# Layer 1's output projection for tokens 0 to 1015 as seven quarter products, and empty side steps ahead of the modulation's column sums

## The chip, the cores and the metric

One core of a Trainium2 chip runs the whole program. The metric is device microseconds of one execution. Before the change the median of three runs is 2443.7 us (2438.36 to 2445.88).

## The reference

A stream x of 2048 tokens with 1024 features passes two layers and a final RMSNorm, all in float32. Each layer computes `h = rmsnorm(x) * (1 + scale) + shift`, a mixer of width 2048 on h, and adds `gate * y`. Shift, scale and gate (3072 numbers a layer) are `silu(c) @ ada_w[i] + ada_b[i]`.

- Layer 0: `u, v, gate = split(h @ w_in)`, then `y = (gelu(u) * spatial(layernorm(gelu(v))) * silu(gate)) @ gmlp_w_out`, where spatial mixes tokens inside chunks of 128.
- Layer 1: `p, gate = split(h @ w_in)`, p has its windowed mean (2, 4, 8 or 16 tokens) taken off, is mixed within four groups and scaled, and `y = (mixed * silu(gate)) @ pool_w_out`.

`pool_w_out` is 2048 x 1024. Its product for the first 1016 tokens is what the change touches.

## The kernel before

**Data.** Features lie on the 128 partitions and tokens on the free axis. Every float32 product is three matmuls (`mm3`, L103) of a high and a low fp32r part: hi*hi, hi*lo, lo*hi. `put` (L109) makes the two parts of a 512-wide piece with one ACT cast (L111) and one DVE subtraction (L112), into one of 9 pairs of tiles.

**Passes.** The tokens are worked in two passes of 1024. A layer's input projection in a pass is 8 groups c of two *units*, and a unit (`unit`, L677) is seven products of quarters (Strassen-like: two halves of the tokens times two halves of the output features, with sums of weights and of rows) of 12 matmuls 128x512 each. Layer 0's stages are the fused weights (`fuse`), `v_phase`, `b_phase0` (L928, both units plus the spatial mixing, PE tile `psp`) and `c_phase0` (L1036), each of the last three once a pass. Layer 1's are `b_phase1` (L1143) and the output projection.

**The two forms of the output projection.** `c_pairs` (L999) serves layer 0: a pass has seven products (order CORDER = 1, 2, 6, 5, 7, 3, 4), each of 8 steps k, each step 4 output blocks times 3 matmuls: 672 matmuls. A step's operands (a piece of y or of a sum of y's quarters, and a piece of weights or of a sum of weights) are two loads into one `raw` tile and two `put`s. After each product four DVE instructions (L1014) add the bank, times the gate, onto the fetched rows of x. The sums of y's quarters are made in `row_sums` (L921), those of the weights in `sum_quarters` (L733: four loads, four DVE subtractions, four stores, all loads and stores on POOL's queue). `c_phase` (L970) serves layer 1's first 1016 tokens: two calls of 508 tokens with all 16 pieces c, 8 output blocks and 3 matmuls: 384 matmuls a call, 768 together. There y's piece is read into a `g` tile. The remaining 1032 tokens go through a third form at the end that the change leaves alone.

**Side steps.** Work that has no place of its own waits in a queue `side`. In `b_phase0` and `b_phase1` the queue is served after every product: one step after each of the 7 products of the first unit, two after each of the second, so 21 a group and 168 a pass. From the second group on, the first step of a group in `b_phase0` is the `row_sums` of the group before, which leaves 161 for the queue. What is left after the last group is run at once by `do_side()` (L958), ahead of `c_phase0`. A `rest` is a step that does nothing.

**The modulation's column sums.** `ada_late` (L470) computes 512 of the 3072 numbers in ten steps: one that issues the first load; eight that each multiply one loaded 128x512 piece of `ada_w` (tile `x`, two of them) by a number of c and add it to `ra` (one tile; L454, L456, DVE); and `last`, in which PE adds up the partitions with 8 matmuls into a bank `pm` (L462) and DVE adds the bias (L464). The loads go on SP's queue behind the weight stream. Pass 0 of `b_phase0` holds five such groups behind 54 steps of RMS norms and 56 of `sum_quarters`, pass 1 three behind 72.

**Order.** Each engine has one list of instructions, fixed when the program is compiled: by and large the order of the text, where an instruction whose operands or buffers are not there yet in the compiler's reckoning lets later ones pass. The stream of weight loads (`Stream`, L33) makes pieces four jobs ahead and loads LEAD (4, in `c_pairs` 8) jobs beyond, as far as `raw` tiles are free: 6 in layer 0, 4 in layer 1.

The functions that the diff touches:

Of the kernel before, what the change touches and what calls it, by code (L numbers as in the profile page):

```python
# [17 lines left out]
P = 128  # L18
# [45 lines left out]
def hybrid_kernel(ctx: ExitStack, tc: tile.TileContext, a: dict):  # L64
# [13 lines left out]
    v_d = dram.tile([2, 8, P, 8, 2 * P], F32, name="v_d")  # L78
    y_d = dram.tile([2, 8, 7, P, TB], F32, name="y_d")
    to_d = dram.tile([8, 2, P, W2], F32, name="to_d")  # L80
    y1_d = dram.tile([NC, P, L], F32, name="y1_d")
    bt_d = dram.tile([8, P, 2 * P], F32, name="bt_d")

    BIG = {"A": 6, "V": 4, "Q": 2, "X": 2}
# [7 lines left out]
    def work(tag, width=512):  # L92
        return wk.tile([P, WK[tag][0]], F32, name=tag, tag=tag, bufs=WK[tag][1])[:, 0:width]
# [4 lines left out]
    def part(pair, *idx):  # L98
        return tuple(t[idx] for t in pair)
# [23 lines left out]
    def st_load(dst, src):  # L123
        st.last = nc.sync.dma_start(dst, src).ins

    def load(dst, src):

        with tc.issue_after(st.last):
            nc.sync.dma_start(dst, src)

    def new_pair():
        return (pair_pool.tile([P, 512], F32R, name="whi", tag="whi"),
                pair_pool.tile([P, 512], F32R, name="wlo", tag="wlo"))
# [4 lines left out]
        return RAW["pool"].tile([P, W2], F32, name="raw", tag="raw")  # L138

    def split(src):  # L140
        p = new_pair()
        put(p, src)
        return p

    def half_jobs(src, step=W2):

        box = []

        def load():
            box.append(raw_tile())  # L150
            for o in range(0, W2, step):
                st_load(box[0][:, o:o + step], src()[:, o:o + step])

        return (load, lambda: split(box[0][:, 0:512])), (None, lambda: split(box[0][:, 512:W2]))
# [138 lines left out]

    CORDER = (1, 2, 6, 5, 7, 3, 4)

    def co_jobs(y, w, t):

        src = {1: lambda k: w(k, 0)[:, 0:512], 2: lambda k: w(k, 1)[:, 0:512], 3: lambda k: w(k, 1)[:, 512:W2],
               5: lambda k: t[k, 0][:, 0:512], 7: lambda k: t[k, 0][:, 512:W2],
               4: lambda k: t[k, 1][:, 0:512], 6: lambda k: t[k, 1][:, 512:W2]}  # L300

        def two(k, pn):
            box = []

            def load():
                box.append(raw_tile())
                st_load(box[0][:, 0:512], y(k, pn))
                st_load(box[0][:, 512:W2], src[pn](k))

            return (load, lambda: split(box[0][:, 0:512])), (None, lambda: split(box[0][:, 512:W2]))  # L310

        return {pn: [st.add(*two(k, pn)) for k in range(8)] for pn in CORDER}

    def c_jobs(y, w):

        jobs = []
        for c in range(0, NC, 2):
            h = [half_jobs(lambda c=c: w[c]) for c in (c, c + 1)]
            i = st.add(y(c), h[0][0], y(c + 1), h[1][0], h[0][1], h[1][1])
            jobs.append(((i[0], i[2]), (i[1], i[3]), (i[4], i[5])))  # L320
        return jobs

    def c0_jobs(pb):
        return co_jobs(lambda k, pn: y_d[pb, k, pn - 1], lambda k, h: a["g_wo"][2 * k + h], to_d)

    def y1_job(c, t0, n, pair):
        box = []

        def load():
            box.append(work("g", n))  # L330
            st_load(box[0], y1_d[c, :, t0:t0 + n])

        def make():
            p = pair()
            put(p, box[0])
            return p

        return load, make

    def c1_jobs(t0, n):  # L340
        return c_jobs(lambda c: y1_job(c, t0, n, lambda: part(new_pair(), every, slice(0, n))), a["p_wo"])

    def c2_jobs(t0, n):

# [29 lines left out]
        return [two_units(unit_jobs_made(c, partial(wf, c)),  # L374
                          unit_jobs(lambda kh, c=c: a["p_wg"][c, kh]), False) for c in range(8)]

    FIRST = ((0, 508), (508, 508))
    jpg = [pg_jobs()]
    jc1 = [c1_jobs(*s) for s in FIRST]
    jpg.append(pg_jobs())  # L380
    jc2 = [c2_jobs(*s) for s in LAST]

# [42 lines left out]
    def ahead(n, fetch, places=2):  # L425

        got = []

        def get(i):
            while len(got) < min(n, i + 1 + places):  # L430
                got.append(fetch(len(got)))
            return got[i]

        return get
# [33 lines left out]
        return [partial(row, 0)] + [partial(step, k) for k in range(KD)] + [last]  # L468

    def ada_late(i, *gs):  # L470
        return [f for g in gs for f in ada_steps(i, g, 4, lambda: work("x"), lambda: work("ra"))]

    def rsqrt(out, v, tmp):
        pw, cols = v.shape
# [492 lines left out]
            nc.scalar.activation(t, po, AF.Copy, scale=g)  # L967
            nc.vector.tensor_add(x, x, t)

    def c_phase(jobs, t0, n, x_src, gate, tag, store):  # L970

        st.ahead = 4
        po = []
        pace = (len(side) + NC - 5) // (NC - 4)

        def fetch(d):
            x = work("x" if d % 4 < 2 else tag, n)
            load(x, x_src[d, :, t0:t0 + n])
            return x

        row = ahead(KD, fetch, 4)
        for c2, (iy, *iw) in enumerate(jobs):
            for d in range(KD):
                if c2 == 0:
                    po.append(bank("po"))
                for j in range(2):
                    w, y = st.get(iw[d // 4][j]), st.get(iy[j])
                    mm3(po[d][:, 0:n], part(w, every, slice((d % 4) * P, (d % 4 + 1) * P)), y,
                        c2 + j == 0, c2 + j == NC // 2)
                if d % 4 == 3:  # L990
                    do_side(pace)
            if c2 == NC // 2 - 2:
                row(0)
        for d in range(KD):
            x = row(d)
            residual(d, x, po[d][:, 0:n], gate)
            nc.gpsimd.dma_start(store[d, :, t0:t0 + n], x)

    def c_pairs(jobs, tokens, n, x_src, gate, tiles, store):  # L999

        st.ahead, st.LEAD = 4, 8
        total, steps = len(side), 0
        xs, pa, pv = {}, [], []

        def fetch(h, nh, tags):
            for i in range(4):
                x = work(tags[i], n)
                nc.gpsimd.dma_start(x, x_src[nh * 4 + i, :, tokens[h]:tokens[h] + n])
                xs[h, nh, i] = x

        def onto(h, nh, banks, last):
            for i in range(4):
                d, x = nh * 4 + i, xs[h, nh, i]
                nc.vector.scalar_tensor_tensor(x, banks[i][:, 0:n], gate[:, 16 + d:17 + d], x, ALU.mult, ALU.add)  # L1014
                if last:
                    nc.gpsimd.dma_start(store[d, :, tokens[h]:tokens[h] + n], x)

        use = {1: ((0, 0), 0), 2: ((0, 0), 1), 6: ((0, 1), 0), 5: ((1, 1), 0), 7: ((1, 1), 1), 3: ((0, 1), 1), 4: ((1, 0), 1)}
        begin = {1: 0, 6: 0, 5: 1, 4: 1}
        for pn in CORDER:  # L1020
            chain = pa if pn in (1, 6, 7, 4) else pv
            if pn in (1, 2, 5):
                chain[:] = [bank("po") for _ in range(4)]
            for k in range(8):
                y, w = (st.get(i) for i in jobs[pn][k])
                for i in range(4):
                    mm3(chain[i][:, 0:n], part(w, every, slice(i * P, (i + 1) * P)), part(y, every, slice(0, n)),
                        k == 0, k == 7, pn in (6, 7, 4, 3))
                if k == 3 and pn in begin:
                    fetch(*use[pn][0], tiles[begin[pn]])  # L1030
                steps += 1
                do_side(total * steps // 56 - (total - len(side)))
            onto(*use[pn][0], chain, use[pn][1])
        st.LEAD = 4
# [3 lines left out]


    tsum = [sum_quarters(t_d[c], partial(wf, c)) for c in range(8)]  # L1040
    tsum_o = [sum_quarters(to_d[k], lambda h, k=k: a["g_wo"][2 * k + h]) for k in range(8)]


# [21 lines left out]
    for b in (0, 1):  # L1065
        rms, steps = fetched_rms(src1(b), TB, "ra", "x", 8)
        rms1.append(rms)
        side.extend(steps)
    side.extend(ada_late(1, 12, 16, 20))
    b_phase0(1, rows, stats)  # L1070
    rows = Rows(1, [src1(0), src1(1)], rms1)
    sums = rows.sum_steps(lambda: work("g"))
# [53 lines left out]
            w *= 2  # L1126
        return steps + [last]

    def gated(bb, c, pc, g1, g2):

        s, y = psc[:, c:c + 1], pc[:, 16:W2 + 16]
        n2 = TB - 8 if bb == 0 else TB
        nc.vector.scalar_tensor_tensor(y[:, 0:TB], y[:, 0:TB], s, g1, ALU.mult, ALU.mult)
        nc.vector.scalar_tensor_tensor(y[:, TB:TB + n2], y[:, TB:TB + n2], s, g2[:, 0:n2], ALU.mult, ALU.mult)
        if bb == 0:
            nc.gpsimd.tensor_copy(keep_g[:, c, :], g2[:, n2:TB])
            nc.gpsimd.dma_start(y1_d[c, :, 0:W2 - 8], pc[:, 16:W2 + 8])
        else:
            e = pc[:, 8:16]
            nc.vector.scalar_tensor_tensor(e, e, s, keep_g[:, c, :], ALU.mult, ALU.mult)  # L1140
            nc.gpsimd.dma_start(y1_d[c, :, W2 - 8:L], pc[:, 8:W2 + 16])

    def b_phase1(bb, rows):  # L1143
        st.ahead = 4
        for c in range(8):
# [25 lines left out]
            g = unit(rows, jpg[bb][c][1], gt, gate)  # L1171
            for pn in ORDER:
                g(pn, 2)
            side.extendleft(partial(gated, bb, c + 8 * i, pcs[i], gt[i], gt[2 + i]) for i in (1, 0))
        do_side()

    def final_out(rms, x, d, t0, n, eng):
# [19 lines left out]
        return wide.pop()  # L1197

    sums = rows.sum_steps(half_wide)
    side.extend(sums[:8])  # L1200
    c_phase(jc1[0], *FIRST[0], x1_d, mod[1], "g", x2_d)
    side.extend(sums[8:])
    c_phase(jc1[1], *FIRST[1], x1_d, mod[1], "g", x2_d)

    def final_steps(t0, n):

# [100 lines left out]
```

## Time and profile before

| | us |
|---|---|
| median of the runs | 2443.7 |
| lowest, highest | 2438.36, 2445.88 |
| the profiled execution | 2437.09 |
| its span | 2435.3 |
| PE busy in it | 2391.0 |
| DVE busy in it | 1932.7 |

The span runs from the first to the last instruction; 1.8 us of the profiled execution lie around it. Times of the trace are microseconds from the span's start. `b_phase0` lies at 280 to 638 and 950 to 1292, `c_phase0` at 642 to 798 and 1292 to 1444, `b_phase1(0)` at 1444 to 1753, the two calls of `c_phase` at 1753 to 1929, `b_phase1(1)` at 1929 to 2237.

### The profile page before, as it was taken

Reading aid. Unit: us, or ns where it says so; the run is one execution under the profiler, and the core shown is the slowest. Engines: PE = TensorE matmul, PEld = TensorE weight load, DVE = VectorE, ACT = ScalarE, POOL = GpSimd, SP = SyncE. Lnnn points to the kernel's source line nnn. Section 1 sums busy time; section 2 is a strip of 40 time slices with the busy share of each in tenths; the row PEclk is TensorE's granted clock in tenths of the full one; section 3 lists DMA queues with packets and bytes.
Section 4 is the critical chain, followed back from the end, with each engine's and each line's share of the span. In section 5 each row is a group of like instructions: output and inputs, shape, how many; then the busy total and the mean of one; then the engine's idle time right before and its main releaser. Section 6 shows DMA issues by size and latency. Waiting matters only on the chain.

```text
span 2435.3 us, 33160 instructions
## 1 busy us (share of the span) xinstructions
PE 2391.0 (98%) x11200; PEld 2014.6 (83%) x11200; DVE 1932.7 (79%) x3231; ACT 1089.4 (45%) x1878; POOL 338.2 (14%) x622
## 2 busy tenths in 40 slices
PE   8999999989999999999999999999999999999998
PEld 7768888868788888888888888888888888888998
DVE  6786789988897677888978869888875498988655
ACT  5744554433465444444446643333354333323533
POOL 2211112321101242010101011010001001100011
PEclk9999999999999999999999999999999999999999
DMA  9733445776778566345536874332566545446664
GB/s 353 260 127 122 144 141 182 240 236 211 259 252 283 183 228 220 135 161 180 172 129 230 259 236 139 121 117 87 165 185 222 179 142 181 143 130 176 224 194 144
DMA packets 191706, 456.21 MB, mean 187 GB/s; under 512 B 24736, under 2 KB 49312, under 8 KB 190512
## 3 DMA queue, kind: packets, MB, share of 16 engines
q1 hardware_dynamic: 148176, 314.02, 40.6%
q0 software_dynamic: 39328, 135.33, 15.5%
q10 hardware_dynamic: 4032, 4.75, 0.6%
q8 instruction: 88, 1.44, 0.3%
q14 instruction: 82, 0.67, 0.1%
HBM read 343.93 MB, written 110.07 MB: 186 GB/s over the span
## 4 chain that ended last, share of the span: by engine, by line
PE 84%; DVE 6%; DMA 6%; issue 2%; ACT 1%; SPq 0%; POOL 0%; DVEq 0%; POOLq 0%; ACTq 0%
PE pu L105 15%; PE pu L107 15%; PE pu L106 15%; PE po L105 9%; PE po L107 9%; PE po L106 9%; PE pa L105 2%; PE pa L106 2%; PE pa L107 2%; PE psp L908 2%; PE pv L107 1%; PE pv L105 1%; PE pv L106 1%; DVE wlo L112 1%; DMA x<-in_ada_w 1%
## 5 line engine op out<-in xcount | busy, mean ns | idle before, releaser
L111 ACT CAST whi<-raw 128x512 fp32r<-128x512 f32 x912 | 539.0, 617 | 614.7 <-PE pu L106 224.5
L112 DVE TENSOR_TENSOR wlo<-raw,whi 128x512 fp32r<-128x512 f32 x912 | 606.0, 686 | 172.4 <-ACT whi L111 167.2
L105 PE MATMUL pu<-S,whi 128*128 128x512 f32 x1024 | 401.0, 392 | 0.0
L107 PE MATMUL pu<-S,wlo 128*128 128x512 f32 x1024 | 398.7, 389 | 0.0
L106 PE MATMUL pu<-S,whi 128*128 128x512 f32 x1024 | 398.5, 389 | 0.0
L105 PE MATMUL pu<-A,whi 128*128 128x512 f32 x768 | 301.3, 392 | 0.0
L107 PE MATMUL pu<-A,wlo 128*128 128x512 f32 x768 | 300.0, 391 | 0.0
L106 PE MATMUL pu<-A,whi 128*128 128x512 f32 x768 | 299.7, 390 | 0.0
L105 PE MATMUL po<-whi 128*128 128x512 f32 (+1 forms) x704 | 275.4, 391 | 0.5 <-ACT whi L111 0.5
L107 PE MATMUL po<-whi,wlo 128*128 128x512 f32 (+1 forms) x704 | 275.2, 391 | 0.3 <-DVE wlo L112 0.3
L106 PE MATMUL po<-wlo,whi 128*128 128x512 f32 (+1 forms) x704 | 275.0, 391 | 0.0
L107 PEld LDWEIGHTS pu<-S,wlo 128*128 128x128 f32 x1024 | 192.2, 188 | 40.2
L105 PEld LDWEIGHTS pu<-S,whi 128*128 128x128 f32 x1024 | 192.3, 188 | 39.1
L106 PEld LDWEIGHTS pu<-S,whi 128*128 128x128 f32 x1024 | 192.3, 188 | 39.0
L107 PEld LDWEIGHTS pu<-A,wlo 128*128 128x128 f32 x768 | 144.7, 188 | 30.4
L106 PEld LDWEIGHTS pu<-A,whi 128*128 128x128 f32 x768 | 145.0, 189 | 29.9
L105 PEld LDWEIGHTS pu<-A,whi 128*128 128x128 f32 x768 | 145.1, 189 | 29.8
L107 PEld LDWEIGHTS po<-whi,wlo 128*128 128x128 f32 x704 | 132.7, 189 | 29.0 <-DVE wlo L112 1.0
L105 PEld LDWEIGHTS po<-whi 128*128 128x128 f32 x704 | 132.9, 189 | 28.4 <-ACT whi L111 0.9
L106 PEld LDWEIGHTS po<-wlo,whi 128*128 128x128 f32 x704 | 132.9, 189 | 27.9
L105 PE MATMUL po<-big,whi 128*128 128x388 f32 (+1 forms) x384 | 123.2, 321 | 0.0
L106 PE MATMUL po<-big,whi 128*128 128x388 f32 (+1 forms) x384 | 122.8, 320 | 0.0
(253 smaller groups left out, 4007.9 us busy)
## 6 DMA issues: line engine op xcount, KB each, us to landing
raw<-y_d SPq DMA_DIRECT2D x112, 256.0 KB, 3.6
raw<-in_p_wo SPq DMA_DIRECT2D x96, 256.0 KB, 3.2
v_d<-g POOLq DMA_DIRECT2D x64, 256.0 KB, 2.8
raw<-in_g_wu SPq DMA_DIRECT2D x32, 512.0 KB, 4.4
raw<-in_g_wg SPq DMA_DIRECT2D x32, 512.0 KB, 4.5
raw<-v_d SPq DMA_DIRECT2D x32, 512.0 KB, 4.6
y_d<-s POOLq DMA_DIRECT2D x64, 256.0 KB, 2.7
x<-in_ada_w SPq DMA_DIRECT2D x64, 256.0 KB, 3.0
```

Of the source, the lines that this page charges most:

```text
L105: nc.tensor.matmul(out, w[0], x[0], start=first and not onto, stop=False, skip_group_check=onto)
L106: nc.tensor.matmul(out, w[0], x[1], start=False, stop=False, skip_group_check=onto)
L107: nc.tensor.matmul(out, w[1], x[0], start=False, stop=last, skip_group_check=onto)
L111: nc.scalar.copy(pair[0], src)
L112: nc.vector.tensor_sub(pair[1], src, pair[0].bitcast(F32))
L908: nc.tensor.matmul(p[:, t * P:(t + 1) * P], vt[h][:, t * 2 * P + j * P:t * 2 * P + (j + 1) * P], bw[:, 0:P], start=True, stop=True)
```

## The change

`c_phase` and its jobs go. Layer 1's first 1016 tokens use `c_pairs` with 508 tokens a half. For that, `gated` also makes the sums of y's quarters and stores seven pieces of 508 columns instead of one of 1016; the sums of `pool_w_out`'s quarters (`tsum_p`, 8 times `sum_quarters`) enter the side queue of `b_phase0(1)`, 7 steps each. The raw tiles of layer 1 stay four. And in `ada_late`, four empty steps stand ahead of each `last`.

```diff
-    y1_d = dram.tile([NC, P, L], F32, name="y1_d")
+    y1_d = dram.tile([8, 7, P, TB - 4], F32, name="y1_d")
+    y2_d = dram.tile([NC, P, W2 + 8], F32, name="y2_d")
+    tp_d = dram.tile([8, 2, P, W2], F32, name="tp_d")
...
     def split(src):
-        p = new_pair()
+        p = part(new_pair(), every, slice(0, src.shape[1]))
...
-                st_load(box[0][:, 0:512], y(k, pn))
+                st_load(box[0][:, 0:n], y(k, pn))
...
-    def c1_jobs(t0, n):
-        return c_jobs(lambda c: y1_job(c, t0, n, lambda: part(new_pair(), every, slice(0, n))), a["p_wo"])
+    def c1_jobs():
+        return co_jobs(lambda k, pn: y1_d[k, pn - 1], lambda k, h: a["p_wo"][k + 8 * h], tp_d, TB - 4)
...
-    jc1 = [c1_jobs(*s) for s in FIRST]
+    jc1 = c1_jobs()
...
-        return [f for g in gs for f in ada_steps(i, g, 4, lambda: work("x"), lambda: work("ra"))]
+        return [f for g in gs for t in (ada_steps(i, g, 4, lambda: work("x"), lambda: work("ra")),)
+                for f in t[:-1] + [rest] * 4 + t[-1:]]
...
+    tsum_p = [sum_quarters(tp_d[k], lambda h, k=k: a["p_wo"][k + 8 * h]) for k in range(8)]
...
-    side.extend(ada_late(1, 12, 16, 20))
+    side.extend(spaced(tsum_p) + ada_late(1, 12, 16, 20))
...
-    def gated(bb, c, pc, g1, g2):
+    def gated(bb, c, pc, g1, g2, first, tiles):
...
-            nc.gpsimd.dma_start(y1_d[c, :, 0:W2 - 8], pc[:, 16:W2 + 8])
+            if c < 8:
+                return
+            n, k = TB - 4, c - 8
+            y11, y21, y12, y22 = (p[:, 16 + h * n:16 + (h + 1) * n] for p in (first, pc) for h in range(2))
+            t = [x[:, 0:n] for x in tiles]
+            for pn, out, p, q, op in ((1, y11, None, None, None), (2, y12, None, None, None), (4, y22, None, None, None),
+                                      (5, t[0], y21, y22, ALU.add), (6, t[1], t[0], y11, ALU.subtract),
+                                      (7, t[2], y11, y21, ALU.subtract), (3, t[3], y12, t[1], ALU.subtract)):
+                if op is not None:
+                    nc.vector.tensor_tensor(out, p, q, op)
+                nc.gpsimd.dma_start(y1_d[k, pn - 1], out)
...
-    side.extend(sums[:8])
-    c_phase(jc1[0], *FIRST[0], x1_d, mod[1], "g", x2_d)
-    side.extend(sums[8:])
-    c_phase(jc1[1], *FIRST[1], x1_d, mod[1], "g", x2_d)
+    side.extend(sums)
+    c_pairs(jc1, [t0 for t0, n in FIRST], FIRST[0][1], x1_d, mod[1], (("g",) * 4, ("x", "x", "ra", "th")), x2_d)
```

## Rows read from the trace of the kernel before

**Rows 1.** The page: busy time of each engine and its share of the span.
```profile
PE 2391.0 (98%) x11200; PEld 2014.6 (83%) x11200; DVE 1932.7 (79%) x3231; ACT 1089.4 (45%) x1878; POOL 338.2 (14%) x622
```
**Rows 2.** What PE waited for: us in total, times, longest.
```profile
PE pm L462 <- DVE ra L456: 12.9, 2, 10.5
...
PE pm L462 <- ACT g L945: 2.8, 1, 2.8
...
PE po L105 <- ACT whi L111: 0.5, 1, 0.5
```
**Rows 3.** Stretches of layer 0's projections and c_phase: us, busy, PEclk, DMA share, GB/s.
```profile
642.50:797.50 155.00, 155.00 (x674) 128.15 (x675) 128.82 (x209) 88.64 (x155) 15.99 (x30) 0.98 0.80 267
1292.00:1444.20 152.20, 152.20 (x673) 125.99 (x673) 125.53 (x204) 89.00 (x156) 16.70 (x31) 1.00 0.77 254
1752.60:1928.90 176.30, 175.56 (x770) 144.03 (x769) 104.64 (x167) 83.07 (x145) 9.31 (x22) 1.00 0.63 193
```
**Rows 4.** PE's timeline at three column sums of b_phase0(0), with the idle time before.
```profile
544.45 1.87 PE L462 MATMUL pm<-ones,ra 128*128 128x1 f32 x8 [10.54 <-DVE ra L456]
...
592.76 1.25 PE L462 MATMUL pm<-ones,ra 128*128 128x1 f32 x8 [2.31 <-DVE ra L456]
...
640.97 1.63 PE L462 MATMUL pm<-ones,ra 128*128 128x1 f32 x8 [2.78 <-ACT g L945]
642.46 0.77 PE L105 MATMUL po<-whi 128*128 128x512 f32 x1
```
**Rows 5.** Stretches around those three (columns as rows 3).
```profile
538.80:549.00 10.20, 4.55 (x15) 3.97 (x16) 8.84 (x17) 2.90 (x5) 0.93 (x2) 0.50 0.40 120
...
593.40:596.80 3.40, 3.40 (x11) 2.82 (x11) 2.75 (x6) 0.47 (x1) 1.04 (x2) 0.50 0.38 131
641.20:648.00 6.80, 6.80 (x21) 5.64 (x21) 3.99 (x8) 0.42 (x1) 4.77 (x9) 0.50 0.89 274
```
**Rows 6.** DVE's timeline at the end of b_phase0(0), in the order of its list.
```profile
624.47 0.16 DVE L464 TENSOR_TENSOR mod<-pm,smalls 128x4 f32<-128x4 f32 x1
624.55 0.49 DVE L454 TENSOR_SCALAR ra<-x,cond 128x512 f32<-128x512 f32 x1
...
639.47 0.68 DVE L706 TENSOR_TENSOR g<-g,pu 128x512 f32<-128x512 f32 x1
640.07 0.75 DVE L456 SCALAR_TENSOR_TENSOR ra<-x,cond,ra 128x512 f32<-128x512 f32 x1
```
**Rows 7.** PE's timeline at two column sums of b_phase0(1).
```profile
1153.84 0.95 PE L462 MATMUL pm<-ones,ra 128*128 128x1 f32 x8
...
1171.20 1.02 PE L462 MATMUL pm<-ones,ra 128*128 128x1 f32 x8
```
**Rows 8.** DMA issues: KB each, median us from issue to landing.
```profile
raw<-y_d SPq DMA_DIRECT2D x112, 256.0 KB, 3.6
...
x<-in_ada_w SPq DMA_DIRECT2D x64, 256.0 KB, 3.0
raw<-to_d SPq DMA_DIRECT2D x64, 256.0 KB, 4.1
```
**Rows 9.** DVE's timeline at the first column sum of b_phase0(0).
```profile
543.65 0.75 DVE L456 SCALAR_TENSOR_TENSOR ra<-x,cond,ra 128x512 f32<-128x512 f32 x1
544.31 0.68 DVE L706 TENSOR_TENSOR g<-g,pu 128x512 f32<-128x512 f32 x1
```
**Rows 10.** Groups of layer 0's c_phase0(1): busy us, mean ns, idle before.
```profile
L112 DVE TENSOR_TENSOR wlo<-raw,whi 128x512 fp32r<-128x512 f32 x110 | 70.5, 687 | 13.8 <-ACT whi L111 13.8
L111 ACT CAST whi<-raw 128x512 fp32r<-128x512 f32 x111 | 62.2, 617 | 27.0 <-PE po L106 23.5 <-issue 2.9 <-PE pu L106 0.7
```
**Rows 11.** One group c of b_phase0(0), b_phase0(1), b_phase1(0), b_phase1(1) (columns as rows 3).
```profile
423.00:465.00 42.00, 42.00 (x204) 35.43 (x204) 39.29 (x67) 18.22 (x30) 16.69 (x31) 1.00 0.78 255
1094.00:1138.00 44.00, 44.00 (x220) 37.23 (x219) 37.13 (x64) 18.99 (x31) 3.79 (x7) 1.00 0.52 172
...
1482.00:1521.00 39.00, 39.00 (x177) 32.41 (x176) 34.57 (x60) 13.57 (x23) 6.92 (x12) 1.00 0.41 141
2160.00:2199.00 39.00, 39.00 (x174) 32.30 (x173) 38.61 (x62) 13.17 (x23) 2.11 (x6) 1.00 0.45 143
```
**Rows 12.** SP's queue in c_phase0(1): what it waited for, us in total, times, longest.
```profile
SPq L124 <- DVE wlo L112: 76.6, 46, 3.5
```

More of the change, by code (lines that the diff above doesn't have):

```diff
@@ L294, in hybrid_kernel, with co_jobs @@
     CORDER = (1, 2, 6, 5, 7, 3, 4)
-    def co_jobs(y, w, t):
+    def co_jobs(y, w, t, n):
         src = {1: lambda k: w(k, 0)[:, 0:512], 2: lambda k: w(k, 1)[:, 0:512], 3: lambda k: w(k, 1)[:, 512:W2],
@@ L306, in load @@
                 box.append(raw_tile())
-                st_load(box[0][:, 0:512], y(k, pn))
+                st_load(box[0][:, 0:n], y(k, pn))
                 st_load(box[0][:, 512:W2], src[pn](k))
-            return (load, lambda: split(box[0][:, 0:512])), (None, lambda: split(box[0][:, 512:W2]))
+            return (load, lambda: split(box[0][:, 0:n])), (None, lambda: split(box[0][:, 512:W2]))
         return {pn: [st.add(*two(k, pn)) for k in range(8)] for pn in CORDER}
[L314 to L321, printed above, removed]
     def c0_jobs(pb):
-        return co_jobs(lambda k, pn: y_d[pb, k, pn - 1], lambda k, h: a["g_wo"][2 * k + h], to_d)
+        return co_jobs(lambda k, pn: y_d[pb, k, pn - 1], lambda k, h: a["g_wo"][2 * k + h], to_d, TB)
     def y1_job(c, t0, n, pair):
@@ L330, in load @@
             box.append(work("g", n))
-            st_load(box[0], y1_d[c, :, t0:t0 + n])
+            st_load(box[0], y2_d[c, :, t0 - W2 + 8:t0 - W2 + 8 + n])
         def make():
@@ L375, in pg_jobs @@
                           unit_jobs(lambda kh, c=c: a["p_wg"][c, kh]), False) for c in range(8)]
-    FIRST = ((0, 508), (508, 508))
+    FIRST = ((0, TB - 4), (TB - 4, TB - 4))
     jpg = [pg_jobs()]
-    jc1 = [c1_jobs(*s) for s in FIRST]
+    jc1 = c1_jobs()
     jpg.append(pg_jobs())
@@ L968, in residual @@
             nc.vector.tensor_add(x, x, t)
[L970 to L997, printed above, removed]
     def c_pairs(jobs, tokens, n, x_src, gate, tiles, store):
@@ L1026, in c_pairs @@
                 for i in range(4):
-                    mm3(chain[i][:, 0:n], part(w, every, slice(i * P, (i + 1) * P)), part(y, every, slice(0, n)),
+                    mm3(chain[i][:, 0:n], part(w, every, slice(i * P, (i + 1) * P)), y,
                         k == 0, k == 7, pn in (6, 7, 4, 3))
@@ L1140, in gated @@
             nc.vector.scalar_tensor_tensor(e, e, s, keep_g[:, c, :], ALU.mult, ALU.mult)
-            nc.gpsimd.dma_start(y1_d[c, :, W2 - 8:L], pc[:, 8:W2 + 16])
+            nc.gpsimd.dma_start(y2_d[c], pc[:, 8:W2 + 16])
     def b_phase1(bb, rows):
@@ L1173, in b_phase1 @@
                 g(pn, 2)
-            side.extendleft(partial(gated, bb, c + 8 * i, pcs[i], gt[i], gt[2 + i]) for i in (1, 0))
+            side.extendleft(partial(gated, bb, c + 8 * i, pcs[i], gt[i], gt[2 + i], pcs[0], gt) for i in (1, 0))
         do_side()
```

## The prediction

> **What bounds the kernel now.** The page's busy times come first: PE is busy 98% of the span, DVE 79% [rows 1]. So a change pays by taking matmuls off PE or by filling its few holes, and costs where it makes a new hole. The list of what PE waited for shows the holes: the largest is `pm`, the modulation's column sums, 12.9 + 2.8 = 15.7 us [rows 2]. PE's timeline places them in `b_phase0(0)`: 10.54, 2.31 and 2.78 us ahead of the first, third and fifth of five sums [rows 4]. Each has a second price: over these places the granted clock is 0.50, the lower level of 1.2 GHz, for 10.2, 3.4 and 6.8 us, in which PE is busy 4.55, 3.40 and 6.80 us [rows 5]. At 2.4 GHz that work takes half, so half of 14.75, 7.4 us, is lost besides. The column sums cost 15.6 + 7.4 = 23.0 us. Last come the stretches of the output projections: in `c_phase0(1)` 672 matmuls take 152.2 us, in the two `c_phase` calls 768 take 176.3 us, both with PE busy throughout but for some 0.7 us [rows 3].
>
> **Part 1: seven products instead of `c_phase`.** 768 matmuls of 508 columns become 672. One takes 175.56 / 768 = 0.2286 us by the busy time of `c_phase`, and 152.2 / 672 = 0.2265 at 512 columns in `c_phase0(1)` [rows 3]. I take 0.2276, between them: 672 x 0.2276 = 152.9 us. Gain 176.4 - 152.9 = **-23.5 us**; ends -24.2 (at 0.2265) and -22.8 (at 0.2286).
>
> What has to keep up: 112 pieces to cast and subtract instead of 96, 28 DVE additions instead of 16 residuals, and the same row sums of the next stage. `c_phase0(1)` does just that work in the same 152 us: DVE is busy 125.5 us there, the DMA share is 0.77, and PE has no hole [rows 3]. That row is the cover. What differs is the number of `raw` tiles, four for six, which is a rival below. I charge 0.6 us for the start, as much as `c_phase` showed [rows 2, 3].
>
> Ahead of it, `gated` gets four more DVE additions a group, 32 in all at about 0.687 us [rows 10], 22 us over 309 us of `b_phase1(0)`, and 40 more DMA issues on POOL's queue. A group there has DVE at 34.6 of 39 us; with 2.7 more it is at 37.3. In `b_phase1(1)` a group runs with DVE at 38.6 of 39 us and PE full [rows 11]. So I cost it at nothing, and at 1 us if a split comes late. The order of the stores hides too: the last group's first piece can be stored some 6 us after the end (an estimate from six DVE instructions and a landing) and is read at step 7 of the first product, 7 x 2.72 = 19 us in.
>
> **Part 2: `tsum_p` in `b_phase0(1)`.** Eight jobs of four loads, four DVE subtractions and four stores; loads and stores wait on POOL's queue ahead of the `y_d` stores. Pass 0 carries the same jobs (`tsum_o`) at DVE 39.3 of 42 us and DMA 255 GB/s, with PE full; pass 1 has DVE at 37.1 of 44 [rows 11], and 2.75 more a job fit. By itself it costs nothing. But its 56 side steps count, in part 4.
>
> **Part 3: the empty steps, where they work.** The first sum's last accumulation ends at 544.4 us, 10.5 us after product 14 of group 5 [rows 9, 4]. Four side steps later is after product 4 of group 6, at 2.72 us a product 10.9 us later. The 10.54 us become about 0.3 with its slow clock gone; the third sum, too, moves off its hole.
>
> **Part 4: the empty steps, where they overflow.** The queue of a pass is served 161 times. Pass 0 now holds 54 + 56 + 5 x 14 = 180 steps, so 19 are left: the fourth group's empty steps and its sum, and the whole fifth group. Pass 1 holds 72 + 56 + 3 x 14 = 170, so 9 are left: four accumulations, four empty steps and the third sum. `do_side()` runs these at once, behind the last product and ahead of `c_phase0`'s first matmul. Then no product stands between an accumulation and its sum.
>
> Does PE's list let `po` matmuls pass the waiting sum? In the trace the fifth sum stands ahead of the first `po`, although its last accumulation (640.07) is behind the last product's addition (639.47) in DVE's own list [rows 6, 4]: the order was kept where the sum could not be ready. I think a matmul that opens a new bank isn't let past one that was to open its bank before. So I take it that PE waits out both chains.
>
> *Length of a chain.* From the fourth sum's addition (624.47) to the fifth sum (640.97) it takes 16.5 us in pass 0, and the sum itself 1 us ahead of it: 17.5 us [rows 4, 6]; from one sum to the next in pass 1 it takes 17.4 us [rows 7]. `ra` is one tile, so a chain cannot start earlier. With DVE free of the products' work it is shorter: 1.1 us to the first step, 0.5 for it, then three turns of load and accumulation, 3 x (3.0 + 0.75) [rows 8, 6], and 0.75: 13.6 us. I take 15.5.
>
> *Pass 0.* The fourth group is now one product later against the end than the fifth was, so its sum waits 2.78 + 2.72 = 5.5 us; the fifth follows 15.5 us later, less 1.3 us of the sum itself: 19.7 us of hole. With 3.4 us for the slow clock, as after 640.97 [rows 5], and 0.3 from part 3, pass 0 loses 23.4 us where it lost 23.0: **+0.4 us**. Ends: 19 and 31 us, so -4 to +8.
>
> *Pass 1.* The second sum falls behind product 12 of the last group. Two products, 5.4 us, remain, then PE waits for the rest of 15.5 us: a hole of 10 us, and 3 us of slow clock [rows 5]: **+13.0 us**, where there is no loss now. Ends: 9 (chain of 13.6) and 17.5 (a slower chain under load).
>
> **Sum.** -23.5 + 0.6 + 0.4 + 13.0 = **-9.5 us**. The profiled execution's 2437.1 would become 2427.6; it stands 6.6 us below the median of the runs, to which the difference is applied: 2443.7 - 9.5 = 2434.2, say **2434 us**. The case's own range, from its ends without all of them together, is 2425 to 2446.
>
> **Rivals.** *PE's list lets `po` pass.* If the compiler puts the late sums some dozens of matmuls into `c_phase0`, the overflow costs only what the chip is behind its reckoning, 1 to 3 us a sum with slow clock, some 6 us in all. Then -23.5 + 0.6 - 23.0 + 0.3 + 6 = -39.6: 2404 us. For it: POOL's and DVE's lists do show later work ahead of earlier. Against it: rows 6. Chance 0.19.
>
> *Four raw tiles starve the pairs (slower).* Place: SP's queue in the new projection. Even with six tiles SP waits 76.6 us in `c_phase0(1)` for a subtraction to free one [rows 12]. With four, a tile must come round within four steps of 12 x 0.2276 us, 10.9 us. It needs two landings beside each other, about 4.1 us and 0.8 to issue [rows 8], and two casts and subtractions one after the other, 0.617 + 2 x 0.687 us [rows 10], 6.9 us together, and the wait of these in DVE's list. That wait decides from 4 us on; 10 us have been seen (product 14's addition at 544.31, its matmuls done by 533.91) [rows 9, 4], but in `b_phase0`, not in a projection. At a round of 12.5 us the 56 steps take 0.40 us more each, 22.6 us: +13.1, 2457 us. Chance 0.08. The Trainium skill (DMA: Bandwidth & Descriptors, Rules for kernel authors) speaks against the change here, as it asks for 1 MiB or more a transfer, and the new loads are 254 KB where weights came in 512. From that page's table (138 GB/s at 64 KB, 341 at 1 MB) an estimate halfway is 240 GB/s, by which the new projection's 38.7 MB (254 GB/s over 152.2 us) would take 161 us and the sum would be -1. The trace does not agree: 256 KB transfers moved 254 GB/s at a share of 0.77 in `c_phase0(1)` [rows 3].
>
> *The empty steps move nothing.* They issue no instruction; if the lists follow readiness alone, the first sum's hole stays. Then the sum is +3.5 us with 2.3 us of slow clock, 2447 us. All sums stand at the product that the count of side steps gives, so 0.05.
>
> **How the numbers follow.** The forecast has 0.68. A measurement of this kernel can tell about 0.3%, 7.3 us, from no change. The forecast's -9.5 with some 6 us to either side gives 0.42 faster, 0.23 same, 0.03 slower of its 0.68; the second case is all faster, the third all slower, the fourth same. Together faster 0.61, same 0.28, slower 0.11. The range that leaves out 2 in 10 reaches into half of the second case and over the fourth: 2403 to 2447.
>
> **What would show it.** Right: one stretch of 672 `po` of 508 columns in about 153 us in layer 1; the 10.54 us before the first `pm` gone; at the end of `b_phase0(0)` two holes of some 5 and 14 us ahead of `pm`, at the end of `b_phase0(1)` one of some 10, each followed by PEclk 0.50. Wrong: `po` matmuls ahead of the last `pm` (then the gain is near 40 us); PE waiting for `whi` or `wlo` all through the new projection (then it is slower).

## The result, and the profile after

| us | before | after |
|---|---|---|
| median of the runs (five each, taken in turn) | 2439.42 | 2455.37 |
| lowest, highest | 2436.73, 2445.88 | 2453.57, 2457.92 |
| the profiled execution | 2437.09 | 2457.92 |
| its span | 2435.3 | 2456.1 |

The changed kernel is slower: ratio 1.0061, interval 1.0042 to 1.0079, and 16.0 us by the medians. It lies above the predicted range. The page's first part and the list of what PE waited for, of the kernel after (line numbers are its own; the sum is now L455, an accumulation L449):

```profile
PE 2377.2 (97%) x11104; PEld 2001.3 (81%) x11104; DVE 1989.5 (81%) x3323; ACT 1093.2 (45%) x1886; POOL 406.7 (17%) x742
...
PE pm L455 <- DVE ra L449: 47.9, 4, 18.9
...
PE po L109 <- DVE wlo L114: 1.9, 3, 1.1
```

PE is busy 13.8 us less than in [rows 1], as 96 matmuls are gone, and yet the span is 20.8 us longer. The wait for `pm` has grown from 15.7 us [rows 2] to 47.9. PE's timeline of the same kernel, at its four late sums (start, duration, the idle time before in brackets):

```profile
635.00 1.84 PE L455 MATMUL pm<-ones,ra 128*128 128x1 f32 x8 [9.71 <-DVE ra L449]
655.74 1.87 PE L455 MATMUL pm<-ones,ra 128*128 128x1 f32 x8 [18.89 <-DVE ra L449]
657.47 0.77 PE L107 MATMUL po<-whi 128*128 128x512 f32 x1
...
1270.65 1.87 PE L455 MATMUL pm<-ones,ra 128*128 128x1 f32 x8 [3.74 <-DVE ra L449]
...
1326.99 1.84 PE L455 MATMUL pm<-ones,ra 128*128 128x1 f32 x8 [15.57 <-DVE ra L449]
1328.69 0.77 PE L107 MATMUL po<-whi 128*128 128x512 f32 x1
```

In both passes the last sum stands directly ahead of the first `po` of `c_phase0`, and PE idles until `ra` is done. The windows view of the same kernel (stretch, its length, busy PE, PEld, DVE, ACT and POOL, granted clock, DMA share, GB/s) over the new projection, over `c_phase0(0)`, and over the three places with holes:

```profile
1793.30:1949.60 156.30, 155.02 (x674) 125.37 (x673) 126.21 (x204) 89.71 (x157) 21.40 (x37) 1.00 0.81 257
...
657.50:811.80 154.30, 154.30 (x674) 127.60 (x675) 122.60 (x197) 84.45 (x148) 11.91 (x22) 0.99 0.74 242
...
630.60:661.40 30.80, 7.50 (x25) 6.63 (x26) 20.99 (x35) 7.65 (x12) 7.09 (x13) 0.50 0.72 242
...
1268.80:1275.80 7.00, 5.15 (x16) 4.47 (x17) 7.00 (x12) 3.19 (x5) 2.71 (x5) 0.51 0.87 265
...
1316.70:1333.70 17.00, 6.71 (x20) 5.68 (x21) 7.21 (x12) 3.45 (x5) 3.80 (x8) 0.50 0.86 297
```

The projection did what it should: 156.3 us where `c_phase` took 176.3 [rows 3]. The holes cost more than that. In pass 0 they are 9.71 + 18.89 = 28.6 us, and half of the 7.50 us that PE is busy there at clock 0.50 is lost besides: 32.4 us in all, where before it was 23.0. In pass 1 they are 3.74 + 15.57 = 19.3 us, and half of 5.15 + 6.71 us: 25.2 us, where there was nothing. So -20.0 + 9.4 + 25.2 = +14.6 us, against +16.0 by the medians. The profiled executions differ by 20.8; about 4 us of that stand ahead of `b_phase0(0)`, where nothing was changed, 2.5 of them in the fused weights (last section).

The stages, each from its first matmul to the first of the next in PE's timeline, with two experiments beside them:

| us | before | after | d_fit | i_both |
|---|---|---|---|---|
| `b_phase0(0)` | 362.6 | 373.7 | 348.1 | 344.3 |
| `c_phase0(0)` | 155.0 | 154.3 | 157.2 | 160.7 |
| `b_phase0(1)` | 342.1 | 364.7 | 343.0 | 346.3 |
| `c_phase0(1)` | 152.3 | 156.2 | 156.6 | 154.4 |
| `b_phase1(0)` | 308.4 | 308.4 | 310.3 | 310.3 |
| layer 1, first 1016 tokens | 176.3 | 156.3 | 155.7 | 154.8 |

### The profile page after: what moved, and what is told of

It is laid out like the page before. It is cut to its first block, busy times and chain, and to the rows that moved or that the text cites. A ratio compares the mean times of both kernels' runs of the same rounds, so it can differ in the third digit from the quotient of the medians.

```text
span 2456.1 us, 33401 instructions
## 1 busy us (share of the span) xinstructions
PE 2377.2 (97%) x11104; PEld 2001.3 (81%) x11104; DVE 1989.5 (81%) x3323; ACT 1093.2 (45%) x1886; POOL 406.7 (17%) x742
## 4 chain that ended last, share of the span: by engine, by line
PE 74%; issue 9%; DVE 7%; DMA 7%; ACT 1%; POOL 1%; SPq 0%; POOLq 0%; DVEq 0%; ACTq 0%
PE pu L107 13%; PE pu L109 13%; PE pu L108 13%; PE po L109 7%; PE po L107 7%; PE po L108 7%; PE pa L107 2%; PE pa L108 2%; PE pa L109 2%; DVE wlo L114 2%; PE psp L902 2%; PE pv L109 1%; PE pv L107 1%; PE pv L108 1%; DMA raw<-in_pool_wpT 1%
## 5 line engine op out<-in xcount | busy, mean ns | idle before, releaser
L113 ACT CAST whi<-raw 128x512 fp32r<-128x512 f32 (+1 forms) x960 | 564.7, 617 | 616.7 <-PE pu L108 212.5
L114 DVE TENSOR_TENSOR wlo<-raw,whi 128x512 fp32r<-128x512 f32 (+1 forms) x960 | 634.3, 686 | 144.4 <-ACT whi L113 141.4
L109 PE MATMUL po<-whi,wlo 128*128 128x512 f32 (+1 forms) x672 | 264.3, 393 | 2.0 <-DVE wlo L114 1.9
L107 PE MATMUL po<-whi 128*128 128x512 f32 (+1 forms) x672 | 263.6, 392 | 0.0
L108 PE MATMUL po<-wlo,whi 128*128 128x512 f32 (+1 forms) x672 | 263.2, 392 | 0.0
L109 PEld LDWEIGHTS po<-whi,wlo 128*128 128x128 f32 x672 | 127.1, 189 | 32.9 <-DVE wlo L114 6.4
L108 PEld LDWEIGHTS po<-wlo,whi 128*128 128x128 f32 x672 | 127.2, 189 | 26.7
L107 PEld LDWEIGHTS po<-whi 128*128 128x128 f32 x672 | 127.4, 190 | 26.3
```

The lines of the kernel that those rows point to most:

```text
L107: nc.tensor.matmul(out, w[0], x[0], start=first and not onto, stop=False, skip_group_check=onto)
L108: nc.tensor.matmul(out, w[0], x[1], start=False, stop=False, skip_group_check=onto)
L109: nc.tensor.matmul(out, w[1], x[0], start=False, stop=last, skip_group_check=onto)
L113: nc.scalar.copy(pair[0], src)
L114: nc.vector.tensor_sub(pair[1], src, pair[0].bitcast(F32))
```

## The experiments

Ratios are to the kernel before, measured in turn with it on the same chip; diffs are against the kernel after unless said otherwise.

**a_norest: the empty steps taken out again.** It tells the overflow from a load that the new projection would bring.

```diff
-                for f in t[:-1] + [rest] * 4 + t[-1:]]
+                for f in t]
```

> The changed kernel without the four empty steps (the seven products and the weight sums in pass 1 stay). Theory 'overflow': the steps left over at the end of a pass stop PE, because po cannot pass a sum. Then pass 0 has the three holes of the kernel before again (10.5, 2.3 and 2.8 us ahead of pm), and pass 1, which now holds 72 + 56 + 30 = 158 of 161 steps, has no hole behind its last product; one ahead of the first sum, 5 to 12 us, since its steps stand as close to the sum as those of pass 0 did. Time: 2455 - 10 (pass 0) - 13 (pass 1) = about 2432 us. Rival 'load': the 16 MB of weight sums in pass 1 make the ada_w loads late wherever they stand; then pass 1 keeps about 19 us of holes and the time is about 2445 us.

Measured: 2437.3 us (2429.3 to 2441.6), ratio 0.9985 (0.9971 to 0.9998). PE's timeline at pass 1's first sum, and the windows view of the new projection, of a_norest:

```profile
1251.74 1.86 PE L455 MATMUL pm<-ones,ra 128*128 128x1 f32 x8 [9.73 <-DVE ra L449]
```
```profile
1766.10:1920.80 154.70, 153.87 (x673) 125.70 (x672) 126.12 (x204) 89.48 (x156) 21.29 (x37) 1.00 0.82 259
```

The long holes at the ends of the passes are gone (`b_phase0(0)` is back at 362.0 us), so they belong to the empty steps. The projection keeps its gain. But most of that gain isn't seen in the time: with `tsum_p` ahead of them, the first sum of pass 1 waits 9.73 us. `b_phase0(1)` takes 356.5 us instead of 342.1, so `tsum_p` by itself costs some 14 us, with no step left over in that pass (170 - 12 = 158 of 161). The trace shows what holds that group at its start: `sum_quarters` works in the two `x` tiles, in `ra` and in `th`, and the modulation's chain in the same `x` and `ra`. What SP's queue waited for from 1225 to 1236 us, and DVE's timeline at the first step of the chain, of a_norest:

```profile
SPq L131 <- DMA tp_d<-x: 6.1, 1, 6.1
```
```profile
1237.89 0.49 DVE L447 TENSOR_SCALAR ra<-x,cond 128x512 f32<-128x512 f32 x1 [0.83 <-DMA tp_d<-ra]
```

The chain's first load waits until the last weight sum has stored its `x`, and its first step until `ra` is stored. The chain's later loads landed after 2.7 to 3.0 us, so they were not slow. How much of the 9.73 us the late start makes was not separated. In pass 0 of the kernel before, the first group behind `tsum_o` waits for such stores too, 6.8 us in two waits.

**b_rest: the kernel before with the empty steps alone.**

```diff
-        return [f for g in gs for f in ada_steps(i, g, 4, lambda: work("x"), lambda: work("ra"))]
+        return [f for g in gs for t in (ada_steps(i, g, 4, lambda: work("x"), lambda: work("ra")),)
+                for f in t[:-1] + [rest] * 4 + t[-1:]]
```

> The kernel before with the four empty steps alone. Overflow: pass 0 holds 180 steps for 161, so the first three holes go and two of some 10 and 19 us stand ahead of the last two sums, with the clock at 0.50 for some 30 us; pass 1 holds 72 + 42 = 114 and shows no hole. Time: 2439 + 10 = about 2449 us. Rival 'load': without the new weight sums the empty steps only help; then the holes of pass 0 shrink to a few us and the time is about 2420 us.

Measured: 2453.5 us (2451.6 to 2456.0), ratio 1.0056 (1.0034 to 1.0078). PE's timeline at the last two sums of `b_phase0(0)`, of b_rest:

```profile
632.35 1.83 PE L462 MATMUL pm<-ones,ra 128*128 128x1 f32 x8 [10.22 <-DVE ra L456]
653.20 1.87 PE L462 MATMUL pm<-ones,ra 128*128 128x1 f32 x8 [19.01 <-DVE ra L456]
```

The two holes of pass 0 come with the empty steps, whatever layer 1 does. In pass 1 no sum waits here: without `tsum_p` its queue holds 114 steps and nothing is left over.

**c_adafirst: the modulation's groups ahead of the weights' sums.** The steps left over are then those of `sum_quarters`, for which no matmul nearby waits.

```diff
-    side.extend(spaced(tsum_o) + ada_late(0, 16, 20) + ada_late(1, 0, 4, 8))
+    side.extend(ada_late(0, 16, 20) + ada_late(1, 0, 4, 8) + spaced(tsum_o))
...
-    side.extend(spaced(tsum_p) + ada_late(1, 12, 16, 20))
+    side.extend(ada_late(1, 12, 16, 20) + spaced(tsum_p))
```

> The changed kernel with the column-sum groups ahead of the weight-sum jobs in both passes, so that what is left over at the end holds no work for PE. Overflow: no hole ahead of any pm in either pass; at the end of pass 0 the late weight sums hold DVE and may cost up to 10 us at the start of c_phase0. Time: 2455 - 32 - 26 = 2397, up to 2407 us. Load: the loads of ada_w are as late as before against their sums, holes of some 20 us remain in pass 1, and the time stays above 2425 us.

Measured: 2436.1 us (2432.2 to 2438.4), ratio 0.9975 (0.9961 to 0.9988); the expectation was missed by some 30 us. PE's waits, and the windows view of `c_phase0(0)`, of c_adafirst:

```profile
PE po L109 <- DVE wlo L114: 14.6, 7, 5.3
PE po L108 <- DVE wlo L114: 10.3, 3, 4.6
```
```profile
624.00:800.90 176.90, 162.23 (x676) 131.78 (x675) 143.25 (x232) 91.02 (x159) 35.43 (x66) 0.94 0.82 283
```

No sum waits any more, with `tsum_p` still in pass 1 but behind the groups. `b_phase0` takes 342.0 us in pass 0, 20.6 less than before, and 344.3 in pass 1, 2.2 more. But the leftover jobs now stand in DVE's list ahead of the splits that `c_phase0` needs: DVE has 232 instructions there instead of 197, PE waits for `wlo`, and the two stages take 176.5 and 168.7 us. The overflow still costs time here, on DVE instead of in the wait for a sum.

**d_fit: no overflow.** The eight groups are spread over pass 0 (four), pass 1 (two) and `b_phase1(0)` (two), so that every queue has room.

```diff
-                for f in t[:-1] + [rest] * 4 + t[-1:]]
+                for f in t[:-1] + [rest] * n + t[-1:]]
...
+    side.extend(spaced(tsum_o) + ada_late(0, 16, 20, n=2) + ada_late(1, 0, 4, n=2))
...
+    side.extend(spaced(tsum_p) + ada_late(1, 8, 12))
...
+    side.extend(b_phase1_side + ada_late(1, 16, 20, n=2))
```

> The changed kernel with the groups spread so that no queue overflows: four groups with two empty steps in pass 0 (158 of 161 steps), two with four in pass 1 (156 of 161), the last two with two in layer 1's first projection (166 of 168). Overflow: holes ahead of pm under 5 us in all, po right behind the last product in both passes: about 2400 us. Load: holes of 15 us or more remain in pass 1, about 2420 us.

Measured: 2412.8 us (2408.1 to 2413.4), ratio 0.9884 (0.9864 to 0.9903). PE's waits, of d_fit:

```profile
PE po L109 <- DVE wlo L114: 7.5, 7, 2.4
PE pm L455 <- DVE ra L449: 6.1, 3, 3.7
```

The wait for `pm` falls from 47.9 to 6.1 us and the time by some 43. With the groups spread like this the changed kernel is 29 us faster than the kernel before, more than the projection's 20, since pass 0's old holes shrink too: `b_phase0(0)` is 14.5 us shorter than before. The expected 2400 us is missed by 13. The first sum of pass 0 still waits 3.67 us, and the two `c_phase0` are 2.2 and 4.3 us longer than before, with most of the 7.5 us of waits for `wlo` in them.

**e_paced: the same steps left over, but run one by one inside `c_phase0`.** This keeps the count, the work and the order of the groups, and changes where the leftover steps run: the sums no longer stand ahead of the first `po`.

```diff
-        do_side()
+        do_side(1)
+        over.extend(side)
+        side.clear()
...
+                if over:
+                    over.popleft()()
```

> The changed kernel, but what is left over after the row sums at the end of a pass is not run at once: c_phase0 runs one of these steps after each of its steps (2.72 us) instead. The same column sums, the same loads and the same chains, only with products of po between an accumulation and its sum. Theory 'order': PE stops because nothing that opens a bank passes the sum; with po ahead of it the holes of 9.7 and 18.9 us in pass 0 and of 15.6 us in pass 1 go, and the one of 3.7 us ahead of pass 1's first sum stays: 2455 - 32 - 20 = about 2405 us, up to 2415 if DVE, waiting for ada_w, makes splits late. Rival 'work': the overflowing groups cost their time wherever they run, since DVE or the loads cannot carry them beside c_phase0; then c_phase0 gets longer by 15 us or more in pass 0 and the time stays above 2430 us.

Measured: 2418.9 us (2415.4 to 2424.1), ratio 0.9899 (0.9876 to 0.9921). PE's timeline at the two late sums of pass 0, then PE's waits, of e_paced:

```profile
642.68 0.95 PE L455 MATMUL pm<-ones,ra 128*128 128x1 f32 x8
...
683.96 0.95 PE L455 MATMUL pm<-ones,ra 128*128 128x1 f32 x8
```
```profile
PE po L109 <- DVE wlo L114: 9.0, 7, 2.0
PE pm L455 <- DVE s L981: 3.7, 1, 3.7
```

Pass 0's late sums now come 60 and 228 `po` matmuls into the projection and wait for nothing. The `po` matmuls ran through the time in which PE idled before, so their operands were there: what held them was their place in PE's list behind a sum that wasn't ready. The Trainium skill (TensorE: Matmul & The Clock Gate, Step-by-step: what each phase is for) says so too: matmuls stay in program order, and only weight loads are pulled ahead. The 18.89 us agree. The time is 14 us above the expected 2405. With the accumulations among DVE's splits `c_phase0` takes 163 and 165 us, where it took 155.0 and 152.3 before: less than rival 'work' asked for in pass 0, but not nothing. The 3.7 us for `pm` in the list are not the hole that was expected to stay: that one, ahead of pass 1's first sum, fell to 0.84 us. They stand ahead of pass 1's late sum, 188 `po` matmuls into the projection:

```profile
1336.67 1.87 PE L455 MATMUL pm<-ones,ra 128*128 128x1 f32 x8 [3.72 <-DVE s L981]
```

This sum waits not for `ra` but for an addition of the projection that reads a bank (L981). The kernel has eight banks, and two chains of four hold all of them there, so it probably waited for a bank to come free; no run tests that.

**f_three: three tiles for the rows of `ada_w`, two fetched ahead.** It asks whether a chain is long because each load waits for a tile, or because the loads share what the DMA engines move.

```diff
-        row = ahead(KD, fetch, 1)
+        row = ahead(KD, fetch, places)
...
+    turn = deque(("x", "x", "th"))
...
-        return [f for g in gs for t in (ada_steps(i, g, 4, lambda: work("x"), lambda: work("ra")),)
+        return [f for g in gs for t in (ada_steps(i, g, 4, three, lambda: work("ra"), 2),)
```

> The changed kernel with three tiles for the rows of ada_w (the tile th in turn with the two of x) and two rows fetched ahead instead of one. The chain of eight loads and accumulations that PE waits out took 20.7 us with two loads on the way, 2.6 us a step at landings of 3.3 to 6.4 us. If the landing time of a load is what it is (latency), a third load on the way makes a step 1.6 to 2 us: the holes of 9.7 and 18.9 us become about 5 and 13 us, that of pass 1 15.6 becomes about 10; time about 2443 us. If the landings are long because the transfers share the engines with others (bandwidth), they grow with a third and the holes stay within 2 us: 2453 us or more.

Measured: 2444.6 us (2438.4 to 2449.4), ratio 1.0007 (0.9995 to 1.0020). PE's timeline at the end of `b_phase0(0)` and of `b_phase0(1)`, then the DMA issues of 626 to 646 us (KB each, median us to landing), of f_three; last, the issues of the kernel after in the same place, 630 to 656 us:

```profile
627.90 1.84 PE L455 MATMUL pm<-ones,ra 128*128 128x1 f32 x8 [6.54 <-DVE ra L449]
645.56 1.87 PE L455 MATMUL pm<-ones,ra 128*128 128x1 f32 x8 [15.83 <-DVE ra L449]
...
1312.38 1.83 PE L455 MATMUL pm<-ones,ra 128*128 128x1 f32 x8 [16.60 <-DVE ra L449]
```
```profile
x<-in_ada_w SPq DMA_DIRECT2D x4, 256.0 KB, 5.5
s<-in_xT POOLq DMA_DIRECT2D x4, 256.0 KB, 7.4
...
th<-in_ada_w SPq DMA_DIRECT2D x2, 256.0 KB, 5.8
```
```profile
x<-in_ada_w SPq DMA_DIRECT2D x9, 256.0 KB, 3.3
s<-in_xT POOLq DMA_DIRECT2D x4, 256.0 KB, 6.5
g<-in_xT SPq DMA_DIRECT2D x4, 256.0 KB, 5.0
```

The time fits the first forecast (2443 us), the holes fit neither well. Pass 0's two holes are some 3 us shorter each, and the 3.74 us ahead of pass 1's first sum are gone, so the loads were late there. But the last holes are still 15.8 and 16.6 us (pass 1's is even 1 us longer), and the loads take 5.5 to 5.8 us instead of 3.3: a third load in flight mostly makes the others longer. Beside them stand the rows of x that `c_pairs` fetches ahead (`s`, `g`) and the first pieces of the projection. Which of these transfers it is that the chain shares with was not separated.

**g_496: 496 columns a matmul in the new projection**, so without the output of 24 of the 1016 tokens. It asks why 672 matmuls of 508 columns take 156.3 us and not less than 672 of 512.

```diff
-    c_pairs(jc1, [t0 for t0, n in FIRST], FIRST[0][1], x1_d, mod[1], (("g",) * 4, ("x", "x", "ra", "th")), x2_d)
+    c_pairs(jc1, [t0 for t0, n in FIRST], 496, x1_d, mod[1], (("g",) * 4, ("x", "x", "ra", "th")), x2_d)
```

> The changed kernel with 496 columns a half in layer 1's output projection instead of 508; it leaves out the output of tokens 496 to 507 and 1004 to 1015. For the size of one matmul: 508 columns took 0.2276 to 0.231 us where 512 take 0.2265. If the excess belongs to a column count that is no multiple of 16, 672 matmuls of 496 take 672 x 0.220 = 148 us with even spacing. If any count but 512 has it, or if late splits make it, the stretch stays at 152 us or more and the spacing stays uneven.

One execution, 2456.6 us. The windows view of the new projection, of g_496:

```profile
1796.50:1948.30 151.80, 150.14 (x673) 126.02 (x672) 124.82 (x204) 89.11 (x156) 20.51 (x37) 1.00 0.83 262
```

From start to start (where nothing waits) a matmul takes 0.2227 us, nearly always between 0.220 and 0.227. At 508 columns it takes 0.2276, between 0.222 and 0.234; at 512 it is 0.2267, nearly all at 0.226 or 0.227. So 508 columns cost a little more than 512, in agreement with [rows 3]. Neither forecast came: a matmul of 496 columns is cheaper, but not the 0.220 us of the first, and its spacing isn't even. That a count which isn't a multiple of 16 costs extra is not shown, as only these three counts were seen.

**i_both: d_fit with four empty steps in pass 0, and what is then left over paced as in e_paced.** The diff is against d_fit, in part.

```diff
-    side.extend(spaced(tsum_o) + ada_late(0, 16, 20, n=2) + ada_late(1, 0, 4, n=2))
+    side.extend(spaced(tsum_o) + ada_late(0, 16, 20) + ada_late(1, 0, 4))
...
+                if over:
+                    over.popleft()()
```

> The spread of the groups that fits the queues (as in d_fit), with four empty steps for each of pass 0's four groups (166 steps for 161) and the five steps left over, four of them empty and the last a sum, run one after each step of c_phase0. Theory 'order': every sum now has at least four products or steps behind its last accumulation, so the hole of 3.7 us ahead of pass 0's first sum goes with its slow clock and none comes at the end: 2413 - 5 = about 2408 us. If the remaining holes belong to DVE's lag and not to the place of the sum, they come back as waits of pu or po for a subtraction and the time stays at 2413 us.

Measured: 2408.7 us (2405.0 to 2412.2), ratio 0.9854 (0.9831 to 0.9877). PE's waits, of i_both:

```profile
PE po L109 <- DVE wlo L114: 8.8, 8, 3.0
PE pm L455 <- DVE ra L449: 4.1, 2, 3.3
PE pu L107 <- DVE g L690: 1.9, 1, 1.9
```

This is the fastest version: about 33 us below before, and some 47 below after by medians of different series. PE waits 2 us less for `pm` than in d_fit, and some 3 us more for `po` and `pu`. Its interval overlaps d_fit's, which was measured in another series, so which of the two is better stays open.

## Why the prediction was wrong

**Part 1 was nearly right.** Forecast -23.5 + 0.6 = -22.9, measured -20.0. A matmul took the 0.2276 us that I took (153.0 us for 672); the other 3.3 us are late splits and short stalls, 1.3 of them in the wait for `wlo`, where I charged 0.6 for the start. The stage took 154.8 to 156.3 us in the seven profiles with this form (after and all experiments but b_rest and g_496), so 1 to 2 us of the miss vary from profile to profile. Two slips in the working change nothing: `c_phase` took 176.3 us, not 176.4, and 56 x 0.40 is 22.4, not 22.6.

**Part 2 failed.** "By itself it costs nothing" was argued from DVE's and the DMA engines' room in a group. The room was there, and with the groups ahead of `tsum_p` no sum waits (c_adafirst). But `tsum_p` stands ahead of the three groups, and the first of them can't start before the last weight sum has stored the `x` and `ra` that both use. Its sum waits 9.73 us without empty steps, with 14 us lost in the stage (a_norest), and 3.74 us and some slow clock with them. I had counted engine time and steps, and not the tiles; and the effect of the 56 steps I looked for at the end of the queue only.

**Part 3 was right.** The 10.54 us [rows 4] are gone. PE's timeline, after, at that sum:

```profile
548.59 0.95 PE L455 MATMUL pm<-ones,ra 128*128 128x1 f32 x8
549.40 0.80 PE L902 MATMUL psp<-bw,raw 128*128 128x128 f32 x5
```

It stands 0.24 us behind the product before it and waits for nothing.

**Part 4 had the right mechanism and the wrong sizes; this is the step that failed.** Which steps are left over, that nothing passes a waiting sum, how many holes there are at the ends of the passes and the clock of 0.50 behind them came as said. The rival in which `po` passes fell: the sums stand ahead of the first `po`, and e_paced shows what it would have been worth. But "length of a chain", taken at 15.5 us, is 635.00 to 655.74, so 20.7 us; in pass 1 the last two sums stand 22.1 us apart. The working had 13.6 us as its low end, 17.5 seen, and I took a value between the two, lower than what the trace showed, on the ground that DVE would be free. DVE was mostly free, but it was not the limit. DVE's timeline of the kernel after, behind the first of the two sums, in parts, and the issues on SP's queue in the same stretch:

```profile
636.96 0.48 DVE L447 TENSOR_SCALAR ra<-x,cond 128x512 f32<-128x512 f32 x1
639.35 0.75 DVE L449 SCALAR_TENSOR_TENSOR ra<-x,cond,ra 128x512 f32<-128x512 f32 x1 [1.31 <-DMA x<-in_ada_w]
...
643.23 0.75 DVE L449 SCALAR_TENSOR_TENSOR ra<-x,cond,ra 128x512 f32<-128x512 f32 x1 [2.52 <-DMA x<-in_ada_w]
...
646.58 0.75 DVE L449 SCALAR_TENSOR_TENSOR ra<-x,cond,ra 128x512 f32<-128x512 f32 x1 [2.60 <-DMA x<-in_ada_w]
648.58 0.69 DVE L584 TENSOR_TENSOR g<-g,rrow 128x512 f32<-128x512 f32 x1 [1.25 <-DMA g<-in_xT]
...
654.93 0.75 DVE L449 SCALAR_TENSOR_TENSOR ra<-x,cond,ra 128x512 f32<-128x512 f32 x1 [0.26 <-DMA x<-in_ada_w]
```
```profile
640.13 0.33 SPq L131 DMA_DIRECT2D x<-in_ada_w  x1
640.51 0.48 SPq L126 DMA_DIRECT2D raw<-in_g_wo  x1
641.04 0.53 SPq L131 DMA_DIRECT2D g<-in_xT  x1
644.01 0.33 SPq L131 DMA_DIRECT2D x<-in_ada_w  x1
```

A load is issued as soon as an accumulation has freed its tile (639.35 + 0.75 = 640.10, issued at 640.13), and the accumulation that needs it begins at 646.58: 6.4 us, where I had put a landing at 3.0, the median over the kernel [rows 8], and a turn of two rows at 3.75. Rows of x and pieces of weights for what comes next are issued in the same microseconds (`raw`, `g`), and the instructions on them (L584) enter DVE's list among the accumulations. Four loads in a row, issued from 634.88 to 644.01, landed after 4.4, 5.7, 6.4 and 5.1 us, and the chain's other four after 2.7 to 3.3. So the term to be sized was these slow landings at that place. A median hides them there too: it is 3.3 us in that stretch (f_three), with which the 13.6 would have become 14.5. In pass 0 the holes were forecast as 5.5 and some 14 us (19.7 together) and are 9.7 and 18.9; the first is longer than one product, so the fourth chain, too, ran late. With its clock pass 0 loses 32.4 us, not 23.4, against an upper end of 31. Pass 1 was forecast at 13.0 with an upper end of 17.5, and loses 25.2, of which the overflow's hole, 15.57 us and half of the 6.71 behind it, is 18.9, and the rest Part 2's.

**The sum.** -23.5 + 0.6 + 0.4 + 13.0 = -9.5 became -20.0 + 9.4 + 25.2 = +14.6. Of the 24 us between them 9 are pass 0's chains, 12 pass 1's (6 of them Part 2's), and 3 the projection. Both passes went past their upper ends at once, as both hang on the same kind of chain; I had set the range as if their ends would not come together.

**The other rivals.** Four `raw` tiles did not starve the pairs: PE waited 1.9 us for `wlo` in the whole kernel. The estimate from the table of the Trainium skill (DMA: Bandwidth & Descriptors, Measured), 161 us for the projection at 240 GB/s, isn't borne out either: with its 254 KB loads the stretch moved 257 GB/s and took 156.3 us. More `raw` tiles were not tried. The empty steps did move something: see Part 3. What did come, slower than before, had no rival of its own: the forecast's mechanism with dearer chains.

## What to carry to other kernels

Count a queue of side steps to its end before something is added, and say what runs when it is drained: an empty step isn't free if it pushes a dependent pair past the last cover, and a job put at the head of a queue delays all behind it and holds the tiles that they share. When steps are left over, spread them over the stages that have room (d_fit), or drain them between the matmuls of the next stage (e_paced); putting cheaper work last only moved the wait to DVE (c_adafirst). Size a chain of loads by the slow landings at the place where it will run, not by a median, and let terms that hang on the same resource miss together in the range.

## What the runs showed of the hardware

- The granted clock was 0.50 over the whole stretch of 630.60 to 661.40, 30.8 us, in which PE was busy for 7.5; the first `po` stands at 657.47, so it stayed low for another 3.9 us of work. The two holes, whose sums stand 20.7 us apart, also cost the clock of the little work between them.
- A third 256 KB load in flight shortened pass 0's last chain only from 20.7 to 17.7 us, at a DMA share of 0.83 (f_three, 626 to 646 us), and pass 1's not at all: the median landing went from 3.3 to 5.5 us.
- A matmul of 508 columns was no faster than one of 512 (0.2276 and 0.2267 us), while 496 columns took 0.2227.
- The first stage, the fused weights, took between 106 and 112 us in the ten profiled executions, with its code the same in all; so 4 us between two profiles are no sign of a change there.
